# Low parts of the weights, low parts of u and sums of squares: from GpSimd to VectorE while a chain of norms runs

## The chip, the cores and the metric

The kernel runs on one core of a Trainium2 chip. The metric is the device time of one launch in microseconds, the median of three runs. Five engines have queues of their own, each worked off in order: TensorE (PE in the profile, its weight loads PEld), VectorE (DVE), ScalarE (ACT), GpSimd (POOL) and SyncE (SP), which issues the transfers.

## What is computed

Two transformer blocks of two layers each follow one another on one sequence of 512 tokens of width 1024, in float32 with batch 1. The first block carries 256 context tokens beside them in its first layer; it mixes by latent attention, a Fourier transform and a long convolution, and has a squared-ReLU MLP of width 4096. The second block has an HGRN2 layer, then a dilated attention layer, each with a SwiGLU MLP of width 2816, and it normalises what comes out of each part before it adds it. Every norm is the one below; the places where it stands in the second block are what this document is about.

```python
def rms_norm_2(x, g):
    xf = x.astype(jnp.float32)
    y = xf * lax.rsqrt(jnp.mean(xf * xf, axis=-1, keepdims=True) + NORM_EPS)
    return (y * g.astype(jnp.float32)).astype(x.dtype)
...
    for layer in range(DEPTH):
        ...
        u = rms_norm_2(h, norm_g[layer, 0]) * (1.0 + sc1) + sh1
        ...  # y = HGRN2 mixer of u (layer 0), dilated attention of u (layer 1)
        h = h + (1.0 + g1) * rms_norm_2(y, norm_g[layer, 1])
        u = rms_norm_2(h, norm_g[layer, 2]) * (1.0 + sc2) + sh2
        y = swiglu_ffn(u, ffn_w_in[layer], ffn_w_out[layer])
        h = h + (1.0 + g2) * rms_norm_2(y, norm_g[layer, 3])
```

## The kernel before

Activations lie with features on the 128 partitions and tokens along the free dimension, in 8 tiles of 128 features. Each operand of a large product is held as two float32r tiles, a high part (`hi`, rounded by ScalarE, L118) and a low part (`lo`, the rest, a subtraction of two SBUF tiles, L119). `mm3` (L150 to L155) multiplies them in three matmuls: high by high (L153), weight high by low (L154), weight low by high (L155).

A weight chunk of 128 x 1024 comes through `wchunk`: a transfer into a raw tile `wr` (three buffers), the cast on ScalarE, the subtraction on the engine `lo_eng`, GpSimd where nothing is said. The split weight goes to the ring `w` (three buffers), or, with `extra=True`, to `wx` of an extra ring (five buffers), which is open from the output projection of a mixer to the first product of the next stage and its like. A raw tile is free again when its subtraction is done, a `w` or `wx` tile when the last matmul on it is done.

`gemm` makes a product chunk by chunk. Its first `head` chunks can be made in `parts`: all of them for tokens 0 to 255 (the first half), then all of them again for tokens 256 to 511 (the second half). After a half is done, `after` puts a chain of steps on `self.chain`: the sums of squares are reduced by a matmul with ones (L307), ScalarE and VectorE make the reciprocal root (`stat_rstd`), and then there is one step for each of the 8 feature tiles. `link(3)` takes up to three steps of the chain behind each chunk. So the chain of the first half is written between the chunks of the second half, and the chain of the second half between the chunks of the next product, whose first half needs only what the first chain made. A product with `dep=True` is such a next product: it is the one whose loads lie behind a chain, and it calls `link()` for all that is left before its second half.

Between the second block's stages two norms follow one another in a chain: `resid2` (norm of y, addition to x, new sums of squares: r_t at L1292, x at L1293, the square on ScalarE at L283, the sum at L284), three empty steps, the matmul L307 again, and `modulate` by `norm_to` (md_h at L326, u high by ScalarE at L335, u low by VectorE at L336; for two of eight tiles by the other branch, L331 and L332 on ScalarE and L333 on GpSimd). From block one to block two it is `final_norm` in place of `resid2`. In the second half the sums at L284 are on GpSimd.

A tool places the instructions: each engine's queue is put in order when the program is built, by the order in which the code names them and by estimated times, and it stays fixed on the chip. So the place of L307 among the matmuls, and of a subtraction among the steps of a chain, is set beforehand; an instruction whose input is late holds all that is queued behind it.

Of the kernel before, what the change touches and what calls it, by code (L numbers as in the profile page):

```python
# [18 lines left out]
P = 128  # L19
# [60 lines left out]
class Kern:  # L80
# [60 lines left out]
    def wchunk(self, src, n=1024, parts=P, extra=False, lo_eng=None):  # L141

        nc = self.nc
        raw = self.t(self.ring, [P, 1024], "wr", 3)
        nc.sync.dma_start(raw[:parts, :n], src)
        w = self.hl(self.xring, [P, 1024], "wx", 5) if extra else self.hl(self.ring, [P, 1024], "w", 3)
        w = w[:parts, :n]
        self.split(w, raw[:parts, :n], lo_eng or nc.gpsimd)
        return w
# [21 lines left out]
    def gemm(self, srcs, nk, rhs, segs, evac, head=2, parts=None, after=None, n=1024, bg=0, lead=2, dep=False):  # L171

        srcs = list(srcs)
        seg = segs if callable(segs) else (lambda m: segs)
        parts = [(x,) for x in parts] if parts else [seg(0)]
        short = self.xring is None and parts[-1][-1][1] - parts[-1][0][0] <= C
        load = lambda m, short=False: self.wchunk(
            srcs[m], n, extra=self.xring is not None and m > 2, lo_eng=self.nc.vector if short and m % 3 == 2 else None)
        head = min(head, len(srcs))
        keep = [load(m) for m in range(head)] if self.xring is not None else None
        for part in parts if head else ():
            if dep and part is not parts[0]:  # L190
                self.link()
            m0 = 0
            while m0 < head:
                g = lead if m0 == 0 and part is parts[0] else 1 if after and part is not parts[0] else 2
                ms = range(m0, min(m0 + g, head))
                m0 = ms[-1] + 1
                ws = [keep[m] if keep else load(m, short and part is parts[-1]) for m in ms]
                outs = [[self.psa()[:, : e - s] for s, e in part] for _ in ms]
                for k in range(nk):
                    for w, oo in zip(ws, outs):  # L200
                        for (s, e), o in zip(part, oo):
                            self.mm3(o, w[:, k * P : (k + 1) * P], rhs(k)[:, s:e], k == 0, k == nk - 1)
                for m, oo in zip(ms, outs):
                    for (s, e), o in zip(part, oo):
                        evac(m, s, e, o)
                    if (after or part is parts[-1]) and not (dep and len(parts) > 1):
                        self.bg(bg)
                    self.link(3)
            if after:
                self.link()  # L210
                for s, e in part:
                    self.chain += after(s, e)
        for m in range(head, len(srcs)):
            if dep:
                self.link()
            for (s, e), o in zip(seg(m), self.mtile(self.wchunk(srcs[m], n), nk, rhs, seg(m))):
                evac(m, s, e, o)
            self.bg(bg)

    @contextmanager  # L220
    def extra_ring(self, side="right"):
        with self.pool("xring", side) as p:
            self.xring = p
            yield
            self.xring = None
# [887 lines left out]
    def norm_to(self, pool, key, st, g, m, j, s, e, lag=0):  # L1113

        v = {}

        def first():
            v["r"] = self.stat_rstd(self.stp, self.st[st], D)
            v["g"] = self.cached_gain(key, g, m[:, (j + 1) * KD : (j + 2) * KD])

        def tile(k):
            o = j * KD + k
            self.modulate(pool, self.xk(k, s, e), v["r"], v["g"][:, k : k + 1], m[:, o : o + 1], self.u[k][:, s:e],
                          k % 3 == 2)

        return [lambda: None] * lag + [first] + [lambda k=k: tile(k) for k in range(KD)]

# [127 lines left out]
    def final_norm(self, s, e):  # L1255

        nc = self.nc
        v = {}

        def first():  # L1260
            v["r"] = self.stat_rstd(self.stp, self.st[s], D)
            self.st[s] = self.stat_new(self.stp, e - s)

        def tile(k):
            x = self.xk(k, s, e)
            nc.vector.scalar_tensor_tensor(x, x, self.fin_g[:, k : k + 1], v["r"], op0=ALU.mult, op1=ALU.mult)
            self.stat_add(self.stp, self.st[s], x, nc.gpsimd if s else None)

        return [first] + [lambda k=k: tile(k) for k in range(KD)]

# [4 lines left out]
    def resid2(self, l, j, p, y, sty, s, e):  # L1275

        nc = self.nc
        last = l == 1 and j == 1
        v = {}

        def first():
            o = (3 * j + 2) * KD
            v["r"] = self.stat_rstd(self.stp, sty, D)
            v["g"] = self.cached_gain(("res", l, j), self.ng[l][:, (2 * j + 1) * KD : (2 * j + 2) * KD],
                                      self.m2[l][:, o : o + KD])
            if not last:
                self.st[s] = self.stat_new(self.stp, e - s)

        def tile(k):
            t = self.t(p, [P, C], "r2_t", 3 if last else 2)[:, : e - s]  # L1290
            x = self.xk(k, s, e)
            nc.vector.scalar_tensor_tensor(t, y[:, k, s:e], v["g"][:, k : k + 1], v["r"], op0=ALU.mult, op1=ALU.mult)  # L1292
            (nc.gpsimd if last and k % 3 == 0 else nc.vector).tensor_tensor(x, x, t, op=ALU.add)  # L1293
            if not last:
                self.stat_add(self.stp, self.st[s], x, nc.gpsimd if s else None)
            elif k % 2:
                nc.sync.dma_start(self.a["out"][:, k - 1 : k + 1, s:e], self.x[:, k - 1 : k + 1, s:e])

        return [first] + [lambda k=k: tile(k) for k in range(KD)]
# [20 lines left out]
    def hgrn(self, es_x):  # L1320
        nc, a = self.nc, self.a
# [6 lines left out]
        with ExitStack() as es:  # L1328
# [4 lines left out]
            v = self.t(rp, [P, 4, D], "v")  # L1333
# [2 lines left out]
            nc.vector.tensor_copy(mask, rmask)  # L1336
            nc.sync.dma_start(rmask, a["hg_reset"])

            ws = [[self.wchunk(a["hg_wv"][c, kp], extra=4 * c + kp > 2) for kp in range(4)] for c in range(2)]
            for s, e in HALVES:  # L1340
                if s > 0:
                    self.link()
# [2 lines left out]
                for kk in range(KD):  # L1345
                    for c in range(2):
                        w = ws[c][kk // 2][:, (kk % 2) * 512 : (kk % 2 + 1) * 512]
# [193 lines left out]
    def dilated(self, es_x):  # L1541
        with ExitStack() as es:
            cp = es.enter_context(self.pool("cat"))
            cat = [self.hl(cp, [P, L], f"cat{k}") for k in range(KD)]
            with ExitStack() as hs:
                p = hs.enter_context(self.pool("qk"))
                self.dilated_heads(p, hs, es_x, cat)
            es_x.enter_context(self.extra_ring())
            with self.pool("y") as yp:
                self.proj_out(1, "at_wout", yp, cat)  # L1550

# [456 lines left out]
```

## Time and profile before

| what | value |
|---|---|
| median of 3 runs | 3566.88 us (3566.8 to 3569.93) |
| the profiled execution | 3567.03 us |
| its span, first to last instruction | 3565.2 us |
| TensorE busy | 3305.0 us, 93% |
| VectorE busy | 2122.9 us, 60% |
| ScalarE busy | 1296.0 us, 36% |
| GpSimd busy | 1378.7 us, 39% |
| mean granted TensorE clock | 0.969 of full speed |

Busy time of TensorE runs on while matmuls overlap and while the clock is low, so 93% does not mean that 93% of the span ran at its best pace. 7% of the span it waited for something. The profiled execution is 0.15 us over the median, and 1.8 us of it lie outside the span.

### The profile page before, as it was taken

What the parts mean: (1) busy time and instruction counts of PE and PEld (TensorE: products, weight loads), DVE (VectorE), ACT (ScalarE), POOL (GpSimd) and SP (SyncE); (2) the same over time, 40 slices, a digit from 0 to 9 for tenths busy, and PEclk for the clock granted to TensorE, in tenths of its full rate; (3) what the DMA queues carried; (4) which work ended last, traced back from release to release, by engine and by line L of the source; (5) the groups of instructions that cost most, each with busy time, mean ns of one, the idle gap of its engine ahead of it and who ended that gap; (6) DMA issues with size and microseconds to landing.
All of it is one profiled execution on the core that took longest, in us unless ns stands there. A gap on an engine that the chain in (4) does not pass through costs nothing. (4 is left out here: it accounts for less than half of the span.)

```text
span 3565.2 us, 46665 instructions
## 1 busy us (share of the span) xinstructions
PE 3305.0 (93%) x18232; PEld 2779.7 (78%) x18232; DVE 2122.9 (60%) x3144; ACT 1296.0 (36%) x2278; POOL 1378.7 (39%) x730
## 2 busy tenths in 40 slices
PE   7988988999998988999989898999899999989998
PEld 3776667888886766988877787888788878888887
DVE  7677778575466467757674656476585474461224
ACT  4235634121124346422245555222323323352222
POOL 2424434232234344434443344344433333434443
PEclk9989999999999999999999999999999999989999
DMA  6330044343343210345531123455313223322332
GB/s 207 122 98 26 24 136 122 119 123 122 122 127 95 95 45 30 110 136 188 184 122 57 56 85 93 150 183 186 101 52 101 92 75 100 102 65 89 95 95 71
DMA packets 145344, 374.31 MB, mean 105 GB/s; under 512 B 19515, under 2 KB 28770, under 8 KB 145124
## 3 DMA queue, kind: packets, MB, share of 16 engines
q1 hardware_dynamic: 140900, 367.14, 32.6%
q10 hardware_dynamic: 4224, 4.19, 0.3%
q8 instruction: 143, 2.34, 0.3%
q14 instruction: 77, 0.63, 0.1%
HBM read 364.98 MB, written 6.29 MB: 104 GB/s over the span
## 5 line engine op out<-in xcount | busy, mean ns | idle before, releaser
L119 POOL TENSOR_TENSOR w_l<-wr,w_h 128x1024 fp32r<-128x1024 f32 (+1 forms) x401 | 967.4, 2414 | 1642.5 <-ACT w_h L118 1592.6
L153 PE MATMUL A<-u_h,w_h 128*128 128x512 f32 (+1 forms) x2344 | 879.2, 376 | 12.8 <-ACT w_h L118 3.7
L154 PE MATMUL A<-u_l,w_h 128*128 128x512 f32 (+1 forms) x2344 | 874.9, 373 | 8.0 <-DVE u_l L336 5.5
L155 PE MATMUL A<-u_h,w_l 128*128 128x512 f32 (+1 forms) x2344 | 873.6, 373 | 8.3 <-POOL w_l L119 8.3
L118 ACT CAST w_h<-wr 128x1024 fp32r<-128x1024 f32 (+1 forms) x406 | 420.3, 1037 | 1085.2 <-PE A L154 725.9
L153 PEld LDWEIGHTS A<-u_h,w_h 128*128 128x128 f32 x2344 | 450.3, 192 | 103.4 <-ACT w_h L118 5.8
L155 PEld LDWEIGHTS A<-u_h,w_l 128*128 128x128 f32 x2344 | 450.9, 192 | 91.9 <-POOL w_l L119 10.0
L154 PEld LDWEIGHTS A<-u_l,w_h 128*128 128x128 f32 x2344 | 450.6, 192 | 91.1 <-DVE u_l L336 6.7
L380 DVE SCALAR_TENSOR_TENSOR mo_a<-mo_w,mc_c,mo_a 128x512 f32<-128x512 f32 x308 | 323.4, 1050 | 105.2 <-DMA mo_w<-in_ada_dram 59.4
L155 PE MATMUL A<-hid_h,w_l 128*128 128x512 f32 (+1 forms) x1072 | 376.9, 352 | 8.4 <-POOL w_l L119 8.4
L154 PE MATMUL A<-hid_l,w_h 128*128 128x512 f32 (+1 forms) x1072 | 378.6, 353 | 3.5 <-DVE hid_l L119 3.5
L153 PE MATMUL A<-hid_h,w_h 128*128 128x512 f32 (+1 forms) x1072 | 379.2, 354 | 1.9 <-ACT hid_h L118 1.9
L155 PEld LDWEIGHTS A<-hid_h,w_l 128*128 128x128 f32 x1072 | 203.4, 190 | 38.4 <-POOL w_l L119 10.5
L154 PEld LDWEIGHTS A<-hid_l,w_h 128*128 128x128 f32 x1072 | 203.8, 190 | 31.5 <-DVE hid_l L119 4.7
L153 PEld LDWEIGHTS A<-hid_h,w_h 128*128 128x128 f32 x1072 | 203.5, 190 | 30.1 <-ACT hid_h L118 2.9
L1751 DVE TENSOR_TENSOR sg<-A,sg 128x512 f32<-128x512 f32 (+1 forms) x52 | 31.4, 608 | 242.6 <-PE A L155 209.0
L119 POOL TENSOR_TENSOR wx_l<-wr,wx_h 128x1024 fp32r<-128x1024 f32 x55 | 134.4, 2457 | 79.4 <-ACT wx_h L118 74.7
L1134 DVE SCALAR_TENSOR_TENSOR x<-A,m,x 128x512 f32<-128x512 f32 (+1 forms) x96 | 62.0, 657 | 169.7 <-PE A L155 169.7
L284 DVE TENSOR_TENSOR st_h<-st_h,st_sh 128x256 f32<-128x256 f32 x137 | 108.6, 800 | 56.6 <-ACT st_sh L283 52.6
L1081 DVE TENSOR_TENSOR relu<-relu 128x512 f32<-128x512 f32 (+1 forms) x104 | 83.7, 833 | 82.5 <-ACT relu L1080 82.3
L1583 DVE TENSOR_TENSOR qk<-A,cos 128x512 f32<-128x512 f32 (+1 forms) x56 | 47.0, 841 | 131.0 <-PE A L155 130.8
L153 PE MATMUL A<-w_h,u_h 128*128 128x256 f32 (+1 forms) x408 | 120.7, 296 | 2.1 <-DVE rt L1586 2.1
(553 smaller groups left out, 6264.4 us busy)
## 6 DMA issues: line engine op xcount, KB each, us to landing
wr<-in_w_mlp_dram SPq DMA_DIRECT2D x139, 512.0 KB, 3.7
mo_w<-in_ada_dram SPq DMA_DIRECT2D x192, 256.0 KB, 3.5
wr<-in_ff_win_dram SPq DMA_DIRECT2D x88, 512.0 KB, 3.6
mo_w<-in_w_mod_dram SPq DMA_DIRECT2D x160, 256.0 KB, 3.1
wr<-in_at_wqk_dram SPq DMA_DIRECT2D x48, 512.0 KB, 3.6
wr<-in_ff_wout_dram SPq DMA_DIRECT2D x32, 512.0 KB, 3.6
wr<-in_w_in_dram SPq DMA_DIRECT2D x30, 512.0 KB, 3.6
wr<-in_w_out_dram SPq DMA_DIRECT2D x24, 512.0 KB, 3.6
```

The source lines that it names most:

```text
L118: nc.scalar.copy(dst.hi, src)
L119: (lo_eng or nc.vector).tensor_tensor(dst.lo, src, dst.hi.bitcast(F32), op=ALU.subtract)
L153: ins = mm(out, lhs.hi, rhs.hi, start=first, stop=False)
L154: mm(out, lhs.hi, rhs.lo, start=False, stop=False)
L155: mm(out, lhs.lo, rhs.hi, start=False, stop=last)
L284: (eng or nc.vector).tensor_tensor(acc, acc, sq, op=ALU.add)
L380: nc.vector.scalar_tensor_tensor(state[i], raw, cc[:, k : k + 1], state[i], op0=ALU.mult, op1=ALU.add)
L1081: nc.vector.tensor_tensor(r, r, r, op=ALU.mult)
L1134: nc.vector.scalar_tensor_tensor(x, ps, mod[:, o : o + 1], x, op0=ALU.mult, op1=ALU.add)
L1583: nc.vector.tensor_tensor(d, vw(ps), vw(c), op=ALU.mult)
L1751: nc.vector.tensor_tensor(sgs[s], ps, sgs[s], op=ALU.mult)
```

## The change

Four things change. (1) In a product with `dep=True` the low parts of the head's chunks are made by VectorE, not GpSimd; so are those of the eight chunks of `hg_wv`, which is written out by hand. (2) With an extra ring open, such a product loads its chunks 3, 4 and 5 (which go to `wx`) first, then 0, 1, 2, 6 and 7. (3) `norm_to` no longer uses the branch of `modulate` with ScalarE and GpSimd for tiles 2 and 5, and the sums of squares of the second half are on VectorE. (4) The extra ring that is opened last, before the output projection of the dilated attention, has six buffers; the others stay at five.

```diff
-        w = self.hl(self.xring, [P, 1024], "wx", 5) if extra else self.hl(self.ring, [P, 1024], "w", 3)
+        w = self.hl(self.xring, [P, 1024], "wx", self.xbufs) if extra else self.hl(self.ring, [P, 1024], "w", 3)
...
         load = lambda m, short=False: self.wchunk(
-            srcs[m], n, extra=self.xring is not None and m > 2, lo_eng=self.nc.vector if short and m % 3 == 2 else None)
+            srcs[m], n, extra=self.xring is not None and m > 2,
+            lo_eng=self.nc.vector if dep or short and m % 3 == 2 else None)
         head = min(head, len(srcs))
-        keep = [load(m) for m in range(head)] if self.xring is not None else None
+        keep = None
+        if self.xring is not None:
+
+            order = sorted(range(head), key=lambda m: (m not in (3, 4, 5), m)) if dep else range(head)
+            keep = {m: load(m) for m in order}
...
-            self.modulate(pool, self.xk(k, s, e), v["r"], v["g"][:, k : k + 1], m[:, o : o + 1], self.u[k][:, s:e],
-                          k % 3 == 2)
+            self.modulate(pool, self.xk(k, s, e), v["r"], v["g"][:, k : k + 1], m[:, o : o + 1], self.u[k][:, s:e])
...  (final_norm and resid2)
-            self.stat_add(self.stp, self.st[s], x, nc.gpsimd if s else None)
+            self.stat_add(self.stp, self.st[s], x)
...  (hgrn)
-            ws = [[self.wchunk(a["hg_wv"][c, kp], extra=4 * c + kp > 2) for kp in range(4)] for c in range(2)]
+            ws = [[self.wchunk(a["hg_wv"][c, kp], extra=4 * c + kp > 2, lo_eng=nc.vector) for kp in range(4)] for c in range(2)]
...  (dilated)
-            es_x.enter_context(self.extra_ring())
+            es_x.enter_context(self.extra_ring(6))
```

The products with `dep=True` and a head are the first MLP product of both layers of block one (`w_mlp1`; in its layer 0 the head is 3, loaded once for each part, and there is no extra ring), the first product of both SwiGLU MLPs (`ff_win`), and the queries and keys of the dilated attention (`at_wqk`).

## Rows read from the trace of the kernel before

**Rows 1.** The page's first part: engine, busy us (share of span), instructions.
```profile
PE 3305.0 (93%) x18232; PEld 2779.7 (78%) x18232; DVE 2122.9 (60%) x3144; ACT 1296.0 (36%) x2278; POOL 1378.7 (39%) x730
```

**Rows 2.** Waits of TensorE, 1804 to 3240 us: total us, times, longest.
```profile
PE B L307 <- DVE st_h L284: 35.5, 6, 8.4
PE B L307 <- POOL st_h L284: 13.7, 3, 5.5
...
PE A L154 <- DVE u_l L336: 4.9, 5, 1.5
```

**Rows 3.** Four stretches: length, busy PE, PEld, DVE, ACT, POOL, clock, DMA; their sum.
```profile
2144.10:2237.30 93.20, 77.25 (x587) 74.98 (x586) 61.27 (x106) 45.59 (x98) 36.62 (x22) 0.93 0.30 91
2549.50:2644.90 95.40, 78.05 (x586) 76.27 (x586) 82.22 (x151) 35.54 (x70) 37.11 (x23) 0.89 0.21 66
...
sum 368.90, PE 309.43 PEld 292.86 DVE 256.51 ACT 169.46 POOL 147.54; mean PE 77.36 PEld 73.22 DVE 64.13 ACT 42.36 POOL 36.89
```

**Rows 4.** The same view of TensorE alone, 256 columns, then 512, unhindered.
```profile
2132.30:2143.70 11.40, 11.40 (x97) 1.00 0.47 147
...
1919.00:1929.60 10.60, 10.60 (x47) 1.00 0.03 4
```

**Rows 5.** TensorE in order of time: start, us, what [idle before <- releaser].
```profile
2170.49 0.80 PE L307 MATMUL B<-st_h,ones 128*128 128x256 f32 x1 [8.41 <-DVE st_h L284]
...
3153.02 0.77 PE L307 MATMUL B<-st_h,ones 128*128 128x256 f32 x1 [7.07 <-DVE st_h L284]
```

**Rows 6.** VectorE in order of time, the chain ahead of the wait at 2170.49.
```profile
2152.41 3.02 DVE L1292 SCALAR_TENSOR_TENSOR r_t<-y,gain,st_rh 128x256 f32<-128x256 f32 x2
2155.35 2.94 DVE L1293 TENSOR_TENSOR x<-x,r_t 128x256 f32<-128x256 f32 x2
2158.22 0.87 DVE L1292 SCALAR_TENSOR_TENSOR r_t<-y,gain,st_rh 128x256 f32<-128x256 f32 x2
2159.01 0.74 DVE L1293 TENSOR_TENSOR x<-x,r_t 128x256 f32<-128x256 f32 x2
2159.68 1.08 DVE L284 TENSOR_TENSOR st_h<-st_h,st_sh 128x256 f32<-128x256 f32 x3
...
2161.75 2.96 DVE L1292 SCALAR_TENSOR_TENSOR r_t<-y,gain,st_rh 128x256 f32<-128x256 f32 x2
...
2168.09 3.21 DVE L284 TENSOR_TENSOR st_h<-st_h,st_sh 128x256 f32<-128x256 f32 x3 [0.63 <-ACT st_sh L283]
```

**Rows 7.** GpSimd in order of time, the same stretch.
```profile
2152.47 5.21 POOL L119 TENSOR_TENSOR w_l<-wr,w_h 128x1024 fp32r<-128x1024 f32 x2 [1.91 <-ACT w_h L118]
2161.56 2.48 POOL L119 TENSOR_TENSOR wx_l<-wr,wx_h 128x1024 fp32r<-128x1024 f32 x1 [3.88 <-ACT wx_h L118]
```

**Rows 8.** Line 119 by engine: ns min/median/max, first and last start.
```profile
L119 DVE TENSOR_TENSOR w_l<-wr,w_h x5: 1208/1212/2594, 527.2 to 1112.7; 128x1024 fp32r<-128x1024 f32 x5
...
L119 POOL TENSOR_TENSOR wx_l<-wr,wx_h x55: 2341/2407/2821, 1436.9 to 3514.7; 128x1024 fp32r<-128x1024 f32 x55
```

**Rows 9.** Groups by line and shape, 2190 to 2199.9 us, a second half's sums.
```profile
L284 POOL TENSOR_TENSOR st_h<-st_h,st_sh 128x256 f32<-128x256 f32 x7 | 6.1, 868 | 6.7 <-ACT st_sh L283 6.4
L1292 DVE SCALAR_TENSOR_TENSOR r_t<-y,gain,st_rh 128x256 f32<-128x256 f32 x8 | 5.0, 666 | 0.0
L1293 DVE TENSOR_TENSOR x<-x,r_t 128x256 f32<-128x256 f32 x8 | 4.1, 551 | 0.0
```

**Rows 10.** ScalarE in order of time: casts of the next product's chunks 0 and 3.
```profile
2147.04 1.05 ACT L118 CAST w_h<-wr 128x1024 fp32r<-128x1024 f32 x1 [1.91 <-PE A L154]
...
2160.45 1.03 ACT L118 CAST wx_h<-wr 128x1024 fp32r<-128x1024 f32 x1
```

**Rows 11.** The page's transfers: issues, KB each, us to landing.
```profile
wr<-in_ff_win_dram SPq DMA_DIRECT2D x88, 512.0 KB, 3.6
```

**Rows 12.** TensorE in order of time, first MLP product, layer 0, then 1.
```profile
556.02 0.79 PE L155 MATMUL A<-u_h,w_l 128*128 128x512 f32 x1 [2.56 <-POOL w_l L119]
...
1488.82 0.48 PE L307 MATMUL B<-st_h,ones 128*128 128x256 f32 x1 [2.40 <-DVE st_h L284]
```

More of the change, by code (lines that the diff above doesn't have):

```diff
@@ L220, in extra_ring @@
     @contextmanager
-    def extra_ring(self, side="right"):
+    def extra_ring(self, bufs=5, side="right"):
+        self.xbufs = bufs
         with self.pool("xring", side) as p:
@@ L1294, in tile @@
             if not last:
-                self.stat_add(self.stp, self.st[s], x, nc.gpsimd if s else None)
+                self.stat_add(self.stp, self.st[s], x)
             elif k % 2:
```

## The prediction, made before the kernel was run

> **What bounds the kernel now.** I read the page's busy shares first [rows 1]: TensorE is busy 93% of the span, so elsewhere time can only be won where it waits or runs slowly. The second view is the waits of TensorE over the second block and the change into it, 1804 to 3240 us [rows 2]. The longest entry is not a product but the small matmul L307 that adds the squares of a norm: 35.5 us in six waits for sums made by VectorE, 13.7 us in three for sums made by GpSimd. Low parts of u cost 4.9 us more. Together 54.1 us. The third view is TensorE in order of time [rows 5]: four of the six waits are one event, repeated at each change of stage with two norms in the chain. They come in the second half of the old product, ahead of the second norm of the first half, and last 7.07 to 8.41 us. With the two small ones (4.7 us together) the sum is 35.5, so these four are 30.8.
>
> Why are the sums late? The view of VectorE and that of GpSimd over the same stretch say it [rows 6, 7]. Two r_t take 0.87 us at 2158 but 3.02 at 2152, two x take 0.74 and then 2.94; the long ones lie within a subtraction of GpSimd (5.21 us for two), and end as it ends. The same at 2161.75 (2.96 for 0.87, beside a subtraction of 2.48) and at 2168.09 (3.21 for 1.08). What VectorE lost is 2.15 + 2.20 + 2.09 + 2.13 = 8.57 us, and the wait that follows is 8.41 [rows 5]. So each low part of the next weights that GpSimd makes stops the chain by about 2.1 us. L307 was queued where the chain would have been done without these stops.
>
> The fourth view is the length of the four stretches [rows 3], 368.9 us in all. Unhindered, TensorE issues 97 matmuls of 256 columns in 11.40 us and 47 of 512 in 10.60 [rows 4], so 0.119 and 0.230 us from one to the next. Three stretches hold three halves of 192 matmuls of 256 columns (576 x 0.119 = 68.5 us), the first one such half and 192 of 512 (22.8 + 44.2 = 67.0): 272.6 us. The excess is 96.3 us; 54.1 are the waits above, 42.2 are matmuls at the lower clock level (0.93 and 0.89 granted in the two stretches shown), the norms' own matmuls and small waits.
>
> **The change, part by part.** *Low parts of the weights.* Forty subtractions of full heads (five products of eight chunks) and five of the six in layer 0 of block one (one was VectorE's already) move. Each takes 2.41 us on GpSimd and 1.21 on VectorE, 2.59 in the one case where something stood in its way [rows 8]. GpSimd loses 45 x 2.41 = 108 us, VectorE gains 45 x 1.21 = 54 us of work and loses the stops of about 2.1 us. Neither bounds the kernel by its total [rows 1]; what counts is where the 1.21 us fall. The best end is in VectorE's gaps (while ScalarE makes a root, or before the chain starts): nothing on the path. The worst is ahead of chain steps, the five of a first half all before L307: 5 x 1.21 = 6.1 us of wait in place of 7.07 to 8.41. The code names the chain's steps before the loads, so I expect the chain to go first and three of them to slip in while a step waits for ScalarE: 3.6 us per chain, 14.5 for four. Half of the two small waits (2.4) stay too. Recovered of the 35.5: 35.5 - 14.5 - 2.4 = 18.6 us.
>
> The subtraction waits on VectorE's queue for its cast. That cast waits for a transfer (3.6 us to landing [rows 11]) or for the old product's last matmul on the buffer (the casts at 2147 and 2160 [rows 10]). Behind it on the queue stand the chain's steps, and behind these L307 and TensorE. On GpSimd only other low parts stood behind it.
>
> *Sums of squares of the second half.* In a second half GpSimd is busy 6.1 us with seven sums, while eight r_t and eight x on VectorE take 5.0 and 4.1 us [rows 9]; at the undisturbed pace they would take 3.5 and 3.0 [rows 6]. VectorE loses 2.6 us to the sums on GpSimd and would need 7 x 1.08 / 3 = 2.5 us to make them itself: even. What goes is GpSimd's tail behind the last x, and an order that counted on sums sooner than they came. The bounds are all of the 13.7 us and nothing; I take half, 6.8. The Trainium skill (SBUF — State Buffer, Who interferes with whom) states that the two engines share a port pair that is locked for the whole instruction and that the loser fully blocks; by that rule VectorE would lose up to the 6.1 us, and the three second halves would give back 10.8 us more. The trace shows 2.6 of 6.1, so I go by the row.
>
> *Low parts of u.* Tiles 2 and 5 of a norm go the way of the other six. VectorE has one more pass of the length of an r_t (0.44 us [rows 6]), ScalarE one less, and GpSimd no longer stops VectorE. Between a gain of all 4.9 us of [rows 2] and a like loss I take a gain of half: 2.5.
>
> *Chunks 3, 4 and 5 first.* No transfer is added, but SP's and ScalarE's queues change order. The three raw tiles are now taken by chunks that need a `wx` buffer, and that is free only after the old product's second half has passed its own chunk 3; today chunk 0 is cast after chunk 0 of that half, 13 us earlier [rows 10]. Chunk 0's transfer starts when the subtraction of chunk 3 is done, and needs 3.6 + 1.05 + 1.21 = 5.9 us to its low part [rows 8, 10, 11]. In three products (`w_mlp1` of layer 1, `ff_win` of layer 0, `at_wqk`) the ring has five buffers. In the first the chain is short and the time suffices; in the other two I expect 2.5 us each of wait for chunk 0 (bounds 0 and 5.9): -5.0. The sixth buffer lets the last `ff_win` subtract chunk 3 before the chain and so frees a raw tile in time. Its own cost is memory.
>
> **The sum.** Waits recovered: 18.6 + 6.8 + 2.5 - 5.0 = 22.9 of 54.1 us, 42%. Of the 42.2 us beside them three quarters should follow the waits (after a long wait the matmuls run at the lower level; the norms' matmuls stay): 0.42 x 31.7 = 13.3. In block one [rows 12] the waits of 2.56 and 2.40 us halve: 2.5. In all 38.7, against the profiled execution's 3567.0 (the median is 0.15 lower): **3528 us**. The stretches outside the changes of stage should stay as they are.
>
> **The rivals.** *Low parts on the path.* All eight 1.21 us fall into the chains: first halves keep 24.4 + 2.4, gain 8.7; second halves keep 3 x 3.6, gain 2.8; low parts of u 2.5; chunk 0 -5.0. That is 9.0, 17%, with 5.3 at the clock and 1 in block one: 15 us, **3552**. For it speaks that VectorE is busy 82.2 of 95.4 us in the third stretch [rows 3]; against it, that eight stops of about 2.1 us are up to 17 of these. The Trainium skill (Perfetto Trace Analysis, Optimizing Scalar/DVE Operations) goes this way: where VectorE is saturated, work may be moved off it, even to GpSimd, the reverse of this change; it adds that the shared port may spoil that, and here the stops bear the second part out.
>
> *Everything in the gaps.* No low part on the path and chunk 0 in time: 33.1 + 6.8 + 2.5 = 42.4, 78%, 24.8 at the clock, 3.5 in block one: 71 us, **3496**.
>
> *Slower: TensorE waits for chunk 0 instead.* The mechanism is the raw ring at the three products with five buffers. If the subtraction of chunk 3 stands behind the last step of the first half's chain, chunk 0 starts its 5.9 us only when u is ready, and the first half starts that much after its inputs. That eats the gain at these places and adds 3 x 5.9 = 17.7; if VectorE's added work also eats the gain at the other two, the time is **3585**. It decides from the point at which that subtraction lies behind the chain rather than in the gap at L307.
>
> *No effect.* The planner queues L307 as early as before and the wait only changes its name: **3567**.
>
> **How the numbers follow.** Forecast (3512 to 3542) 0.50, low parts on the path (3542 to 3560) 0.20, everything in the gaps 0.08, no effect 0.09, slower 0.13. Faster is 0.78, the same 0.09, slower 0.13, where 0.2% (7 us) is about what a measurement of this kernel can tell from no change. The range takes in the first three cases, from 3496 to 3562; what it leaves out is the slower case, most of the case without effect and half of the best one.
>
> **What the profile would show.** Right: in the chains' stretches no r_t, x or sum over 1 us beside GpSimd; the four waits at L307 below 4 us; none there for GpSimd; GpSimd busy some 132 us less (108, and 28 sums of 0.87 [rows 9]) and VectorE about as busy as now, since added work and lost stops cancel; the four stretches some 36 us shorter together. Wrong in the step on chunk 0: waits of the first matmuls of `ff_win` or `at_wqk` for `w_h` or `w_l` over 3 us. Wrong in the step on the gaps: subtractions of 1.21 us in a row in front of r_t or x, with L307 waiting. The whole would fall if the waits stayed although VectorE's steps run undisturbed.

## The result, and the profile after

The changed kernel takes 3508.6 us (median; 3504.9 to 3510.5), the one before beside it 3566.8: ratio 0.984, 95% interval 0.982 to 0.985, so 58 us less. The forecast was 39 us less (3528), with 3496 to 3562 as its range. The profiled execution of after is one of 3510.5 us with a span of 3508.7, 56.5 below the span of before. In the code of after the lines stand 6 or 7 further down: the statistics matmul L307 is L314, r_t and x (L1292, L1293) are L1298 and L1299, the sums (L284) L291.

The page's busy shares, which answer [rows 1]:

```profile
PE 3288.9 (94%) x18232; PEld 2765.4 (79%) x18232; DVE 2096.6 (60%) x3245; ACT 1284.8 (37%) x2248; POOL 1216.7 (35%) x629
```

GpSimd is busy 162 us less and VectorE 26 us less, although 45 low parts of weights, the low parts of two tiles of u in each norm and 28 sums have come to VectorE. The waits of TensorE over 1800 to 3240 us (total, times, longest), which answer [rows 2]:

```profile
PE B L314 <- DVE st_h L291: 10.5, 4, 5.6
...
PE A L155 <- DVE w_l L119: 6.2, 2, 4.7
...
PE A L153 <- ACT u_h L342: 2.4, 1, 2.4
...
PE A L153 <- ACT w_h L118: 2.2, 2, 1.7
...
PE A L154 <- DVE u_l L343: 0.6, 1, 0.6
```

35.5 + 13.7 us of waits at the statistics matmul have become 10.5, and there is no row for sums by GpSimd. New are 8.4 us for the first chunks of the new weights (w_l, w_h). The four changes of stage, in the view by windows (ends at the same matmuls as in [rows 3]; columns as there):

```profile
1827.00:1897.20 70.20, 69.69 (x394) 60.48 (x393) 50.47 (x107) 39.41 (x76) 8.31 (x6) 1.00 0.31 94
2121.75:2205.20 83.45, 75.13 (x586) 73.62 (x585) 57.48 (x125) 44.73 (x94) 7.36 (x3) 0.94 0.33 102
2515.50:2600.10 84.60, 74.39 (x588) 72.42 (x587) 77.03 (x170) 34.27 (x66) 7.88 (x4) 0.96 0.24 74
3085.10:3164.05 78.95, 73.85 (x586) 72.37 (x585) 51.87 (x116) 42.33 (x92) 7.36 (x3) 0.96 0.21 64
sum 317.20, PE 293.06 PEld 278.89 DVE 236.85 ACT 160.73 POOL 30.91; mean PE 73.26 PEld 69.72 DVE 59.21 ACT 40.18 POOL 7.73
```

368.9 us have become 317.2, so 51.7 of the 56.5 us were won here, 18.0, 9.8, 10.8 and 13.1. Another 3.7 lie ahead of the first stretch (1830.70 against 1827.00), but that part differs by more from one execution to the next: a second profiled execution of the changed kernel reaches the same matmul about 4.8 us earlier. VectorE, with more to do, is busy 19.7 us less in them: its instructions are no longer stretched by stops, and a stop counts as busy time. The chain that answers [rows 6], VectorE in order of time ahead of the second norm's matmul of `ff_win` of layer 0:

```profile
2135.52 0.87 DVE L1298 SCALAR_TENSOR_TENSOR r_t<-y,gain,st_rh 128x256 f32<-128x256 f32 x2
...
2136.65 0.75 DVE L1299 TENSOR_TENSOR x<-x,r_t 128x256 f32<-128x256 f32 x2
2137.32 1.21 DVE L119 TENSOR_TENSOR wx_l<-wr,wx_h 128x1024 fp32r<-128x1024 f32 x1
...
2138.79 1.21 DVE L119 TENSOR_TENSOR wx_l<-wr,wx_h 128x1024 fp32r<-128x1024 f32 x1
2139.93 1.28 DVE L291 TENSOR_TENSOR st_h<-st_h,st_sh 128x256 f32<-128x256 f32 x3
2141.12 1.22 DVE L119 TENSOR_TENSOR wx_l<-wr,wx_h 128x1024 fp32r<-128x1024 f32 x1
2143.24 1.23 DVE L119 TENSOR_TENSOR w_l<-wr,w_h 128x1024 fp32r<-128x1024 f32 x1 [0.89 <-ACT w_h L118]
```

Two r_t take 0.87 or 0.88 us throughout this chain, two x 0.75. Two low parts stand ahead of the last sums, the others behind, while ScalarE makes the root. The rows of TensorE that answer [rows 5], and the largest new waits:

```profile
2140.40 0.48 PE L314 MATMUL B<-st_h,ones 128*128 128x256 f32 x1 [0.32 <-DVE st_h L291]
...
2168.21 0.79 PE L314 MATMUL B<-st_h,ones 128*128 128x256 f32 x1 [5.63 <-DVE st_h L291]
...
2548.16 0.58 PE L155 MATMUL A<-u_h,w_l 128*128 128x256 f32 x1 [4.69 <-DVE w_l L119]
...
3126.79 0.80 PE L314 MATMUL B<-st_h,ones 128*128 128x256 f32 x1 [4.13 <-DVE st_h L291]
```

8.41 us have become 0.32. The longest waits that remain are those of the second halves (5.63, 4.13) and, at `at_wqk`, of its first chunk (4.69).

### The profile page after: what moved, and what is told of

It is laid out like the page before. It is cut to its first block, busy times and chain, and to the rows that moved or that the text cites. A ratio compares the mean times of both kernels' runs of the same rounds, so it can differ in the third digit from the quotient of the medians.

```text
span 3508.7 us, 46589 instructions
## 1 busy us (share of the span) xinstructions
PE 3288.9 (94%) x18232; PEld 2765.4 (79%) x18232; DVE 2096.6 (60%) x3245; ACT 1284.8 (37%) x2248; POOL 1216.7 (35%) x629
## 5 line engine op out<-in xcount | busy, mean ns | idle before, releaser
L119 POOL TENSOR_TENSOR w_l<-wr,w_h 128x1024 fp32r<-128x1024 f32 (+1 forms) x381 | 917.9, 2411 | 1897.4 <-ACT w_h L118 1862.1
L154 PE MATMUL A<-w_l,u_h 128*128 128x256 f32 (+1 forms) x408 | 119.6, 293 | 0.0
L155 PE MATMUL A<-w_h,u_l 128*128 128x256 f32 (+1 forms) x408 | 118.7, 291 | 0.0
```

The lines of the kernel that those rows point to most:

```text
L119: (lo_eng or nc.vector).tensor_tensor(dst.lo, src, dst.hi.bitcast(F32), op=ALU.subtract)
L154: mm(out, lhs.hi, rhs.lo, start=False, stop=False)
L155: mm(out, lhs.lo, rhs.hi, start=False, stop=last)
```

## The experiments

Times are medians; each ratio is to the kernel before, run on the same chip beside it.

| Kernel | us | ratio (95%) |
|---|---|---|
| changed kernel, again | 3508.4 | 0.984 (0.9825 to 0.9855) |
| before, low parts of the weights on VectorE | 3515.1 | 0.985 (0.984 to 0.987) |
| after, these low parts on GpSimd | 3563.9 | 0.999 (0.998 to 1.000) |
| after, idle subtractions on GpSimd | 3559.7 | 0.998 (0.997 to 0.999) |
| after, idle fills on GpSimd | 3509.7 | 0.984 (0.982 to 0.985) |
| after, sums of second halves on GpSimd | 3524.5 | 0.988 (0.986 to 0.989) |
| after, chunk order 0, 1, 2, ... | 3508.9 | 0.983 (0.982 to 0.985) |
| after, last ring of five | 3509.7 | 0.9835 (0.982 to 0.985) |
| after, low parts of u of tiles 2, 5 on GpSimd | 3501.7 | 0.9815 (0.980 to 0.983) |
| before, weights and sums on VectorE | 3507.9 | 0.984 (0.982 to 0.985) |
| the same, norm's matmul later | 3521.0 | 0.987 (0.986 to 0.989) |
| tiles 2, 5 on GpSimd, norm's matmul later | 3516.7 | 0.986 (0.984 to 0.988) |

**One part alone, and all but that part.** The kernel before with

```diff
-lo_eng=self.nc.vector if short and m % 3 == 2 else None)
+lo_eng=self.nc.vector if dep or short and m % 3 == 2 else None)
...
-extra=4 * c + kp > 2)
+extra=4 * c + kp > 2, lo_eng=nc.vector)
```

> The kernel before with one part of the change: VectorE makes the low parts of the weights of the dependent products and of hg_wv; order of the chunks, ring of five, sums of squares and low parts of u stay as before. Theory (the stops of about 2.1 us that GpSimd's subtractions lay on the norm chains were the cost): the four waits of 7 to 8 us of TensorE at the statistics matmul fall below 3 us each and the kernel gains 35 to 50 us, 3517 to 3532 us, most of the 58 us. Rival (the order of the chunks, the six buffers and the sums carry the gain, the engine of the low parts little): under 20 us, 3547 or more, with the four waits at 5 us or more because chunk 3's subtraction now stands ahead of the chain on VectorE.

and the changed kernel with these lines reversed:

> The changed kernel with the low parts of the weights back on GpSimd; the order 3, 4, 5 first, the six buffers, the sums and the low parts of u stay as changed. Theory of the stops: the four waits at the statistics matmul return to 6 to 8 us each and the kernel loses 30 to 45 us, 3539 to 3554 us. Rival (the other parts carry the gain): within 10 us of the changed kernel, 3500 to 3519.

The first gains 53 us, the second loses 54 to 55 us against the changed kernel. Both are more than expected (35 to 50 and 30 to 45). So the low parts of the weights are the change: alone they bring 53 of 58 us, and everything else together, without them, some 4. Of the waits at the statistics matmul the first kernel shows

```profile
PE B L307 <- POOL st_h L284: 24.4, 4, 8.4
...
PE B L307 <- DVE st_h L284: 1.9, 3, 1.2
```

so the waits for VectorE's sums, 35.5 us before, are 1.9, while the waits for GpSimd's sums have grown from 13.7 to 24.4. In the second kernel the waits are back:

```profile
PE B L314 <- DVE st_h L291: 36.6, 10, 7.5
```

At the four places of the first halves these are 7.5, 3.5, 5.6 and 7.0 us (6 to 8 each were expected); most of the rest is at sums of second halves, which VectorE makes in this kernel. The rival (order, buffers and sums carry the gain) falls by both. Nor do GpSimd's low parts cost time by coming too late themselves: TensorE waits 2.3 + 0.9 us for them in the kernel before, and 2.1 + 0.9 us for those that are left in the changed one.

**The stop itself.** Two runs leave VectorE's instructions as they are in the changed kernel, and give GpSimd work that nobody needs, behind the high part of 40 chunks:

```diff
+if self.xring is not None and lo_eng is nc.vector:
+    for o in (0, 512):
+        h = w.hi[:, o : o + 512].bitcast(F32)
+        nc.gpsimd.tensor_tensor(self.junk, h, h, op=ALU.subtract)
```

> The changed kernel, to which GpSimd has been given idle work: behind each high part of a dependent product's chunk (and of hg_wv) with the extra ring it subtracts that high part from itself, twice 512 columns, into a scratch tile that nobody reads; VectorE's instructions and their order are unchanged. Theory of the stops (GpSimd's two-input work over SBUF stops VectorE's two-input work): the waits at the statistics matmul return to 4 to 8 us at the four places, VectorE's r_t and x show 2 to 3 us beside these subtractions, and the kernel loses 20 to 40 us, 3529 to 3549. Rival (the norm chains were late because of how the instructions were queued, and GpSimd's work beside them is harmless): within 5 us of the changed kernel.

and in the other, in the place of the loop,

```diff
+    nc.gpsimd.tensor_copy(self.junk[:, :1], w.hi[:, :1].bitcast(F32))
+    for _ in range(4):
+        nc.gpsimd.memset(self.junk, 0.0)
```

> As the kernel with GpSimd's idle subtractions, but GpSimd's idle work reads next to nothing: behind each high part it copies one column of it and then fills the scratch tile four times with zeros. If GpSimd stops VectorE whenever it works on SBUF, the loss is like that of the idle subtractions, 51 us in all, as far as the fills take as long: 3530 to 3560 us. If only its reads stop VectorE's two-input work, r_t and x keep 0.4 us beside the fills and the kernel stays within 5 us of the changed one, 3504 to 3514.

Idle subtractions cost 51 us against the changed kernel, more than the 20 to 40 expected and nearly the whole gain of the change; idle fills cost about 1. (Per chunk two subtractions take 2 x 1.10 us in the median, a copy of one column and four fills 0.35 + 4 x 0.53, so GpSimd is at work about as long.) The statistics matmuls stand at the same places in TensorE's order as in the changed kernel, so nothing was queued anew there. But the loss did not come where the theory put it. At the four places of the first halves TensorE waits 4.9, 0.3, 2.5 and 2.0 us, not 4 to 8, and x keeps its pace. With the idle subtractions the waits show

```profile
PE B L319 <- DVE st_h L296: 23.0, 8, 6.4
...
PE A L158 <- DVE u_l L348: 7.1, 2, 4.4
```

against 10.5 us for sums and 0.6 for u_l in the changed kernel; those for u_h, w_h and w_l together are 19.1 against 10.8. In the chain ahead of `ff_win` of layer 0 GpSimd's first subtraction is kept out by VectorE itself (last section), and most steps that stop come later, about the root and behind it, as here (GpSimd's row, then VectorE's):

```profile
2165.67 7.79 POOL L152 TENSOR_TENSOR junk<-w_h 128x512 f32<-128x512 f32 x6
...
2165.80 2.43 DVE L338 SCALAR_TENSOR_TENSOR md_h<-x,gain,st_rh 128x256 f32<-128x256 f32 x2
```

So the run shows that such stops cost what the change gains; that they fall on the steps ahead of the matmul, as in [rows 6], is shown by the kernel with the low parts back on GpSimd, where two r_t at 3140.91 take 2.96 us beside a low part of 2.54, and the matmul behind them waits 6.99. The groups of VectorE's chain steps by line and shape over 1826 to 3230 us (busy us, mean ns of one), of the kernel before,

```profile
L284 DVE TENSOR_TENSOR st_h<-st_h,st_sh 128x256 f32<-128x256 f32 x81 | 59.7, 750 | 41.3 <-ACT st_sh L283 38.5 <-DVE st_h L284 0.5
L1292 DVE SCALAR_TENSOR_TENSOR r_t<-y,gain,st_rh 128x256 f32<-128x256 f32 x48 | 38.4, 834 | 0.2
L336 DVE SCALAR_TENSOR_TENSOR u_l<-md_h,m,u_h 128x256 fp32r<-128x256 f32 x48 | 35.9, 765 | 9.6 <-ACT u_h L335 9.4
```

of the changed one,

```profile
L291 DVE TENSOR_TENSOR st_h<-st_h,st_sh 128x256 f32<-128x256 f32 x107 | 51.4, 490 | 30.6 <-ACT st_sh L290 29.0
L343 DVE SCALAR_TENSOR_TENSOR u_l<-md_h,m,u_h 128x256 fp32r<-128x256 f32 x64 | 30.4, 507 | 4.4 <-ACT u_h L342 4.2
...
L1298 DVE SCALAR_TENSOR_TENSOR r_t<-y,gain,st_rh 128x256 f32<-128x256 f32 x48 | 21.4, 477 | 0.1
```

with the idle subtractions,

```profile
L296 DVE TENSOR_TENSOR st_h<-st_h,st_sh 128x256 f32<-128x256 f32 x109 | 65.2, 609 | 29.3 <-ACT st_sh L295 27.5
L348 DVE SCALAR_TENSOR_TENSOR u_l<-md_h,m,u_h 128x256 fp32r<-128x256 f32 x64 | 38.1, 625 | 2.2 <-ACT u_h L347 2.0
L338 DVE SCALAR_TENSOR_TENSOR md_h<-x,gain,st_rh 128x256 f32<-128x256 f32 x64 | 36.8, 610 | 0.2
...
L1303 DVE SCALAR_TENSOR_TENSOR r_t<-y,gain,st_rh 128x256 f32<-128x256 f32 x48 | 24.6, 543 | 0.1
```

and with the idle fills:

```profile
L296 DVE TENSOR_TENSOR st_h<-st_h,st_sh 128x256 f32<-128x256 f32 x107 | 51.6, 493 | 30.5 <-ACT st_sh L295 28.8
L348 DVE SCALAR_TENSOR_TENSOR u_l<-md_h,m,u_h 128x256 fp32r<-128x256 f32 x64 | 30.4, 507 | 4.1 <-ACT u_h L347 3.7
L338 DVE SCALAR_TENSOR_TENSOR md_h<-x,gain,st_rh 128x256 f32<-128x256 f32 x64 | 28.2, 476 | 0.2
...
L1303 DVE SCALAR_TENSOR_TENSOR r_t<-y,gain,st_rh 128x256 f32<-128x256 f32 x48 | 21.4, 476 | 0.1
```

In the run with fills the mean steps are within 3 ns of those of the changed kernel; in the run with subtractions four kinds of step take 13.6 + 7.7 + 8.6 + 3.2 = 33.1 us more on VectorE (about 1 of it for two more sums in this record). In the kernel before three kinds took 81 x 0.260 + 48 x 0.357 + 48 x 0.258 = 50.6 us more than at the pace of the changed one. So it is not that GpSimd works, but that it works with operands read from the memory that VectorE's two-operand steps read too. That is the statement of the Trainium skill (SBUF — State Buffer, Who interferes with whom) that a VectorE instruction with two SBUF inputs contends with a GpSimd instruction that reads SBUF, and not with one that only writes it; the two runs agree, 3559.7 against 3509.7 us.

**The sums.** In the changed kernel, in final_norm and resid2:

```diff
-self.stat_add(self.stp, self.st[s], x)
+self.stat_add(self.stp, self.st[s], x, nc.gpsimd if s else None)
```

> The changed kernel with the sums of squares of the second halves back on GpSimd. First theory (even trade, as the forecast took it: what VectorE adds it no longer loses to stops, and only GpSimd's tail goes): waits at the statistics matmul for sums by GpSimd, 5 to 8 us at the four second halves where the changed kernel waits 0 to 5.6, and 3 to 10 us more in all: 3512 to 3519. Rival (the second halves are bound by VectorE, which is better off without the sums): the same or up to 5 us less, 3504 to 3509.

It loses 15 to 16 us, more than both theories gave; the first has the right sign and place. TensorE's waits at the matmul are now

```profile
PE B L314 <- POOL st_h L291: 20.7, 4, 7.1
...
PE A L153 <- ACT u_h L342: 6.7, 2, 3.6
...
PE B L314 <- DVE st_h L291: 1.2, 3, 0.5
```

21.9 against 10.5 us, and 6.7 against 2.4 for u_h: together 15.7 more. In the second stretch the way from the second half's first r_t to the matmul takes 10.35 us instead of 8.82.

**Order of the chunks, and the sixth buffer.**

```diff
-order = sorted(range(head), key=lambda m: (m not in (3, 4, 5), m)) if dep else range(head)
+order = range(head)
```

> The changed kernel with the chunks loaded in the order 0, 1, 2, ... as before. First theory (3, 4, 5 first is what delays the first chunks): the waits of 8.4 us for chunks 0 and 1 of at_wqk vanish, nothing of the chains comes back, and the kernel gains 3 to 8 us, 3501 to 3506. Second theory (with the low parts on VectorE the early casts of 3, 4, 5 keep VectorE's queue clear of the chains): the waits at the statistics matmul come back with 3 to 6 us in the first halves, and the kernel loses 5 to 15 us, 3514 to 3524.

```diff
-es_x.enter_context(self.extra_ring(6))
+es_x.enter_context(self.extra_ring())
```

> The changed kernel with the last extra ring of five buffers again. Theory (the sixth buffer lets chunk 3 go ahead of the chain): the first matmuls of the last ff_win wait for w_h and w_l as at at_wqk, 4 to 8 us in all, and the kernel loses 2 to 8 us. Rival (such waits only come in the place of the wait of the second half's statistics matmul, 4.1 us there): within 2 us.

Both are within 2 us of the changed kernel. With the plain order no chunk of `at_wqk` is waited for; in its place TensorE waits later, for the second half:

```profile
2562.59 0.79 PE L314 MATMUL B<-st_h,ones 128*128 128x256 f32 x1 [8.37 <-DVE st_h L291]
```

The waits at the matmul in the second halves are 6.7, 8.4 and 5.4 us, where the changed kernel has 5.6, none and 4.1: 10.6 us more, in exchange for 8.4 less for chunks and 2.0 less for u_h. So each theory on the order was right in one sign and wrong in the time: the waits for chunks vanish, but nothing is gained; waits at the matmul come back, but in the second halves (0.3 us at most in the first), and nothing is lost. With five buffers the wait at the last `ff_win` is 6.3 instead of 4.1 us, and no such wait for chunk 0 as at `at_wqk` appears; 2 us are less than the whole time can tell, so the rival stands.

**Low parts of u.**

```diff
-m[:, o : o + 1], self.u[k][:, s:e])
+m[:, o : o + 1], self.u[k][:, s:e], k % 3 == 2)
```

> The changed kernel with the low parts of u of tiles 2 and 5 back on GpSimd. Theory (each such subtraction stops VectorE's next modulation, and its low part lies behind it): TensorE waits 4 to 6 us in all for u_l by GpSimd, 3511 to 3516. Rival (these waits were made by the weights' subtractions ahead of them on GpSimd's queue, which are gone): within 2 us of the changed kernel.

Neither was right: with tiles 2 and 5 on GpSimd again it is 7 us (0.2%) faster than the changed kernel, at the edge of what can be told (the intervals of the two ratios overlap), with all its runs (3500.5 to 3504.4) below those of the two kernels on the same chip that stand at 3509.7, but for the lowest with five buffers (3503.3). Waits of TensorE for u_l are

```profile
PE A L154 <- POOL u_l L340: 0.8, 2, 0.5
PE A L155 <- DVE w_l L119: 0.7, 1, 0.7
```

and the wait for the low parts of `at_wqk` has gone from 6.2 to 0.7 us: it fits this that VectorE has two steps less ahead of them in each norm, though no run shows it apart. But the four stretches are no shorter by it: between the same matmuls they take 316.6 us in the profiled execution, and 316.9 in that of the changed kernel. What the faster one has won lies ahead of them (it is there at 1817.8 us, two executions of the changed kernel at 1822.3 and 1827.1) and was not traced.

**The two parts, and a later place.** The kernel before with the weights' lines of the first experiment and, in both places of the sums,

```diff
-self.stat_add(self.stp, self.st[s], x, nc.gpsimd if s else None)
+self.stat_add(self.stp, self.st[s], x)
```

> The kernel before with two parts of the change only: low parts of the weights and sums of squares of the second halves on VectorE; chunk order, five buffers and the low parts of u as before. Theory (these two parts are the gain, the low parts of u on VectorE cost 7 us, order and sixth buffer are worth nothing): 3499 to 3505 us. Rival (the order or the sixth buffer is needed once the low parts of u are GpSimd's): 3506 to 3515 us.

Beside it ran the changed kernel:

> The changed kernel itself, beside the three others on the same chip: 3505 to 3512 us.

The two parts are level with the whole change (3507.9 and 3508.4 on one chip), as the rival said in its number. That the 7 us for the low parts of u need the order or the sixth buffer is not shown: the four stretches take 318.5 us with the two parts, against 316.6 and 316.9 us above, so order, sixth buffer and the engine of these low parts together are worth some 2 us there. Then, in norm2, the second half's steps were started later and the matmul tied behind the last one named:

```diff
-self.m2[l], 3 * j, s, e, LAG)
+self.m2[l], 3 * j, s, e, LAG + (10 if s else 0),
+                late=s > 0 and (l, j) != (0, 0))
...
+if late:
+    self.queue(ins, self.last_mm)
```

> The kernel with these two parts, and in block two the statistics matmul of the second half's norm is queued behind 144 matmuls of the new product's first half instead of 96. Theory (the waits that are left come from the place of this matmul, 5.7 us too early in TensorE's queue): the three waits of 3 to 8 us at it vanish, the second half still finds its first tile of u, and the kernel gains 6 to 15 us on the one with two parts: 3487 to 3497. Rival (the chain itself is too long): the wait goes to the second half's first matmuls, for u_h by ScalarE or u_l, and the time stays within 4 us.

> The changed kernel with the low parts of u of tiles 2 and 5 on GpSimd, and the statistics matmul of the second half's norm behind 144 matmuls. By the same theory: 3488 to 3497, since chunk order and the sixth buffer are worth nothing. Rival: 3499 to 3504, as without the later place.

Slower by 13 and 15 us. The moved matmul no longer waits, but TensorE does (the kernel with two parts):

```profile
1876.70 0.79 PE L153 MATMUL A<-w_h,u_h 128*128 128x512 f32 x1 [6.21 <-ACT u_h L337]
...
2170.99 0.58 PE L153 MATMUL A<-u_h,wx_h 128*128 128x256 f32 x1 [7.13 <-ACT sg L230]
...
2566.09 0.58 PE L153 MATMUL A<-u_h,wx_h 128*128 128x256 f32 x1 [8.05 <-DVE rt L1589]
```

The first of these rows is what the rival said, a second half that waits for u_h, and a cost of my edit: the lag also moved the norm ahead of the hgrn products, where there was nothing to win. This stretch is 7.4 us longer (8.0 in the other kernel). The two other rows are not second halves. They are matmuls of the new product's first half, at the very place in TensorE's order where the matmul stood before, and what ends the wait is ScalarE's `sg` and VectorE's `rt`, which empty the result tiles of that first half. These stand in their queues behind the second half's chain: ScalarE ends the last square of it at 2169.24, loads a table and runs `sg` from 2170.55. There and at the last `ff_win` (5.52) the three waits are 20.7 us, where the matmul itself waited 17.5. So the place of the matmul was not the reason; behind its wait stood a second one for the same chain, which neither theory had. The three stretches with these waits are 4.3 us longer together (5.4 in the other kernel).

## Why the prediction was right, and where its terms were off

The mechanism and the sign were right, and so was the view that showed it: [rows 6] against [rows 7], a long r_t that ends as GpSimd's subtraction ends. The idle subtractions show it as a cause by what they cost, though not by where the waits fall. The size was 39 instead of 58 us: 3508.6 lies below the forecast's own band (3512 to 3542) and in the range only because that took in part of "everything in the gaps", which had a chance of 0.08. The terms:

- **Low parts in the first halves' chains**, the term that was mis-sized most. The forecast left 14.5 + 2.4 of 35.5 us; 0.7 are left (10.5 less the 5.63 and 4.13 of second halves). Each 1.21 us ahead of the matmul was counted as wait. In the row view two stand ahead of the last sums, 2.42 us, and the wait is 0.32. The matmul's place in TensorE's queue is only a small part of the reason: counted in the traces it stands 5, 5 and 10 matmuls later in the first, second and fourth stretch (0.6 to 1.2 us at 0.119 each [rows 4]), and 4 earlier in the third, where it does not wait either. For this term the forecast's own better case, everything in the gaps, was nearly the true one.
- **Sums of the second halves.** 6.8 of 13.7 us were to go; 9.8 are left, and the third place is short only because TensorE waits for chunk 0 ahead of it. But sums on GpSimd would not have stayed at 13.7: with the weights' low parts off GpSimd they are 24.4 us (that part alone); that TensorE, no longer held in the first half, comes to them sooner is the likely reason, not a shown one. The step took the two parts as independent. Undoing the sums costs 15 to 16 us; with the 10.8 us that the forecast worked out for a full stop, it would have been 17.6. That this comes near is chance, for the stop is not full: with the sums back on GpSimd and no weights there, eight r_t and eight x take 5.0 and 4.1 us beside seven sums of 6.0 us, as in [rows 9], and 3.6 and 3.1 in the changed kernel. In that chain the trade is nearly even, as forecast: it is 1.5 us longer with the sums on GpSimd, 0.85 of it VectorE's and 0.7 the tail behind the last x. More than half of the loss lies in the first stretch (81.5 instead of 70.1 us) and was not traced.
- **Low parts of u.** The wait for u_l fell from 4.9 to 0.6 us, against 2.4 forecast, but not through this edit: with the weights' low parts alone VectorE's and GpSimd's u_l together cost 2.3. The edit itself, forecast at 2.5 us of gain, is worth nothing in the four stretches; the whole time is 7 us lower without it.
- **Chunk 0.** 5.0 us forecast, 8.4 measured, all at `at_wqk` and none at `ff_win`. Of the 8.4, 2.2 are for casts and 6.2 for low parts. The step on the transfer was wrong: chunk 0 was there, cast at 2539.00, and its low part stood on VectorE behind the steps of two norms and a chunk of the extra ring, until 2546.89 (ScalarE's row, then VectorE's). And it costs nothing in the sum, since the second halves would wait as much longer (plain order).

```profile
2539.00 1.03 ACT L118 CAST w_h<-wr 128x1024 fp32r<-128x1024 f32 x1
...
2543.11 1.22 DVE L119 TENSOR_TENSOR wx_l<-wr,wx_h 128x1024 fp32r<-128x1024 f32 x1
...
2546.89 1.22 DVE L119 TENSOR_TENSOR w_l<-wr,w_h 128x1024 fp32r<-128x1024 f32 x1
```

- **Clock and the rest.** 13.3 forecast. Of the 51.7 us won in the stretches the listed waits explain 54.1 - 11.1 less 8.4 for chunks and about 1.2 more for u_h, 33.4; 18.3 are left, which no run takes apart. The granted clock in the four rows is 1.00, 0.94, 0.96 and 0.96 where it was 0.88, 0.93, 0.89 and 0.89.
- **Block one.** 2.5 forecast. Both waits of [rows 12] are gone, not halved: between the same matmuls the stretches around the first MLP products are 7.7 and 4.1 us shorter. Ahead of the first stretch 3.7 us of this are left, and what comes between scatters by as much.

Of the signs, the missing long steps, the four short waits and the missing waits for GpSimd came as said; GpSimd lost 162 us instead of 132, mostly because the forecast's count left out its 28 low parts of u. VectorE was to stay as busy as it was and lost 26, although the weights alone added 54: so by estimate (26 + 54) over 80 us of its busy time had been stops, far more than the four of one chain that I had counted.

The slower rival (chunk 0) had its sign, a wait of 4.69 us at `at_wqk`, without its price. The rival with low parts on the path fell: 0.7 us are left at the first halves, where it kept 24.4.

## What to carry to other kernels

An engine with spare time is no free place for work, if what it does stops the engine that the path hangs on: compare the duration of the same instruction with and without the neighbour at work before pricing a move. A stop taken out of a chain is worth its whole length where a queue is fixed beforehand, while work put into the chain in its place costs only what finds no gap. And where one part of a change takes a stop away, price the next part on the schedule that is left, not on the old one.

The fastest kernel measured is the changed one with tiles 2 and 5 of the low parts of u on GpSimd: 3501.7 us, ratio 0.9815 (0.980 to 0.983); that it is really faster than the changed kernel is not shown. What TensorE waits for at the changes of stage now is mostly the chain of the second half (5.6 and 4.1 us at both `ff_win`); a later place of its matmul does not help, because the results of the first half are emptied behind the same chain.

## What the runs showed of the hardware

The stop works both ways. Of 512 columns, GpSimd's idle subtraction takes 1.10 us in the median, and up to 5.65 where VectorE's steps follow each other without a gap (min/median/max ns):

```profile
L152 POOL TENSOR_TENSOR junk<-wx_h x50: 1039/1103/5646, 1468.8 to 3160.3; 128x512 f32<-128x512 f32 x50
```

In the other run a copy of a single column, 0.18 us at best, takes up to 4.80, and the fills take 0.69 at most (then the longest copy in order of time; GpSimd's spans are rough in this profile):

```profile
L150 POOL COPY junk<-wx_h x25: 184/354/4802, 1468.7 to 3117.4; 128x1 f32<-128x1 f32 x25
...
L152 POOL MEMSET junk<- x160: 524/527/688, 1468.9 to 3119.8; 128x512 f32 x160
...
2135.53 4.80 POOL L150 COPY junk<-wx_h 128x1 f32<-128x1 f32 x1 [21.35 <-ACT wx_h L118]
```

The Trainium skill (SBUF — State Buffer, SBUF: two separate sides) says of the shared ports that whichever of the two instructions starts first gets them for the whole instruction and the other fully blocks. The rows agree that it works in both directions. That a run of short VectorE steps, which in that record follow each other without a gap from 2127.8 to 2142.0, keeps GpSimd out for 4.6 us goes beyond a single instruction.
